# Turning the mixer's last token half by a transposing DMA instead of on TensorE

## The chip, the cores and the metric

The kernel runs on one core of one Trainium2 chip. The metric is the device time of one execution in microseconds; the median of three runs is taken. Engines are named as in the profile: PE is TensorE (matmuls; PEld its weight loads), DVE is VectorE, ACT is ScalarE, POOL is GpSimd, and SP is the engine whose queue issues most DMAs.

## The reference

The model is an encoder of two layers over 512 tokens of width 1024, in float32. Each layer is a half-step SwiGLU block, a mixer, and another half-step SwiGLU block; a final RMSNorm ends it. Only the mixer matters here:

```python
def mixer(h, w_in, gate_bias, rpb, w_na_out, w_f_out, w_o):
    z = h @ w_in
    ...
    y_na = neighbourhood_attention(q.reshape(shp), k.reshape(shp), v.reshape(shp), rpb) @ w_na_out
    y_f = fourier_mix(uf) @ w_f_out
    g_na = jax.nn.sigmoid(ga + gate_bias[0])
    g_f = jax.nn.sigmoid(gf + gate_bias[1])
    return (g_na * y_na + g_f * y_f) @ w_o
```

The change is about the last line: the gated sum, and its product with `w_o`.

## The kernel before

Every product is done in float32 by splitting each operand into a high and a low part and summing three matmuls (high by high, high by low, low by high). ACT copies the high part out (`whi` for weights, `m1h` and so on for activations), DVE subtracts to get the low part (`wlo`, `m1l`).

Large products are done by Strassen's scheme with seven half-size products, numbered 1 to 7. The gated sum is 512 tokens by 1024 features. It is cut into four quarters: features i = 0 or 1 (512 each) by tokens j = 0 or 1 (256 each). As the product with `w_o` needs the features on the partitions, each quarter is turned from tokens by features into features by tokens; the turned quarter is the tile `mq[i, j]`, in the code m00, m01, m10 and m11. The factors of the seven products are

- 1: m00; 5: m00 - m01; 2: m10; 6: that difference + m11; 7: m01 - m11; 3: m11; 4: m10 - (the factor of 6).

`combo` (L578) makes such a sum on DVE, and `parts` (L332, L333) splits it. `product` runs one of the seven over two weight granules of 12 matmuls each (L521, L522, L524); before a granule `ws.next` prepares weights up to two granules ahead: ACT writes `whi` (L199, or L194 where a sign is turned), DVE writes `wlo` (L202, L195), and some granules are first summed with another one on DVE (L172). `whi` and `wlo` have three buffers each, so a granule's copy waits until PE has done with the granule three before it. `put` (L1833) adds a finished bank of a product to the residual `x` on DVE, bank by bank. The products run in the order 1 (bank pair wA), 5 (wB), 2 (wC), 6 and 7 (both adding on into wA), 3 (into wB), 4 (into wA).

There are two ways to turn a quarter. Those of the first features, m00 and m01, go by DMA: `apart` separates the 16-bit words of the float32 values by two ACT copies (L357, tile `zs`) and issues a transposing DMA on the SP queue (L363, tile `zt`); `joined_words` puts the words together again by two ACT copies (L376). Those of the second features go by PE: `to_channels` runs eight transposes into PSUM (L1511) and two ACT evictions (L1512). The quarter (1, 1), the second features' second token half, is turned in a hook of the product wA, between its two granules; the quarter (1, 0) behind it. Ahead of this, `merge(1, ga1, w, j)` finishes a half: PE multiplies the attention rows with their output weights, DVE multiplies by the gate (L1499) and adds the Fourier part (L1500).

The order on each engine is made by a planner before the run. It lists the instructions in time by its own estimates, the earlier one in the program going first where two are ready. Where the code says `manual_schedule` for an engine, its order is that of the program: here PE and DVE from the product with the factor of 6 to that of 3, so on DVE the update of wC's first bank, the next weight part, the updates of wA's two banks, and so on. Each engine runs its list in order; an instruction that waits holds up those behind it. Weight loads go through the SP queue into nine raw buffers (L148); a load waits until its buffer is free. POOL issues DMAs that add one weight granule onto another (L158, L204).

Of the kernel before, what the change touches and what calls it, by code (L numbers as in the profile page):

```python
# [9 lines left out]
F32 = mybir.dt.float32  # L10
# [5 lines left out]
ALU = mybir.AluOpType  # L16
# [75 lines left out]
def encoder_kernel(  # L92
# [15 lines left out]
    def nm(s):  # L108
        uid[0] += 1
        return f"{s}_{uid[0]}"  # L110

    def slot(dt=F32, s="k", shape=(4, 256)):
        return kp.tile([P, *shape], dt, tag="k", name=nm(s), bufs=23)
# [5 lines left out]
    def bank(s="ps"):  # L119
        return pp.tile([P, T], F32, tag="ps", name=nm(s))  # L120

    def pair(s="ps"):
        return [bank(s), bank(s)]
# [228 lines left out]
    def words_apart(z):  # L352

        s = slot(U16, "zs", (2, 4, 2, P))
        words = z.bitcast(U16).rearrange("p b (q f h) -> p h q b f", q=4, h=2)
        for h in range(2):
            S.activation(s[:, h], words[:, h], AF.Copy)  # L357
        return s

    def turned_words(s):  # L360

        t = slot(U16, "zt", (2, 4, 256))
        nc.sync.dma_start_transpose(  # L363
            out=t.rearrange("p h q (b t) -> p (h q b) t", b=2), in_=s.rearrange("p h q b f -> p (h q b f)")
        )
        return t

    def apart(z):

        return turned_words(words_apart(z))  # L370

    def joined_words(to, t):

        to = to.bitcast(U16).rearrange("p i (t w) -> p w i t", w=2)
        for w in range(2):
            S.activation(to[:, w], t[:, w], AF.Copy)  # L376
# [140 lines left out]
    def late_low(parts, again=False):  # L517


        for ps, lh, ll, rh, _, start, _ in parts:  # L520
            PE.matmul(ps, lh, rh, start=start, stop=False, skip_group_check=again)  # L521
            PE.matmul(ps, ll, rh, start=False, stop=False, skip_group_check=again)  # L522
        for ps, lh, _, _, rl, _, stop in parts:
            PE.matmul(ps, lh, rl, start=False, stop=stop, skip_group_check=again)  # L524

    def product(ps, acts, kts, start, stop=True, again=False, hook=None, by_block=False, ahead=AHEAD):

        h, l, off = acts  # L530
        n = (len(kts) + 1) // 2

        def granule(i, w, b):
            res = []
            for k, kt in enumerate(kts[2 * i : 2 * i + 2]):
                c, z = slice(off + b * P, off + (b + 1) * P), slice(k * T, (k + 1) * T)
                res.append((
                    ps[b], h[:, kt, c], l[:, kt, c], w[0][:, z], w[1][:, z], start and i + k == 0,
                    stop and 2 * i + k == len(kts) - 1,
                ))  # L540
            return res

        if by_block:
            w = [ws.next() for _ in range(n)]
            for b in range(2):
                for i in range(n):
                    late_low(granule(i, w[i], b), again)
            return
        for i in range(n):
            w = ws.next(AHEAD if i < n - 1 and ahead else ahead)  # L550
            if i < n - 1:
                late_low(granule(i, w, 0) + granule(i, w, 1), again)
            else:
                late_low(granule(i, w, 0), again)
                late_low(granule(i, w, 1), again)
            if hook and i == 0:
                hook()
# [19 lines left out]
    def combo(dst, in0, in1, op, s):  # L577
        V.tensor_tensor(dst, in0, in1, op)  # L578
        return parts(dst, s)

    def parts(src, s):
        h, l = slot(F32R, s + "h"), slot(F32R, s + "l")
        split(h, l, src)
        return h, l, 0

    K4 = list(range(4))
# [499 lines left out]
    def stage_mixer(l, norm, nxt):  # L1086
# [310 lines left out]
        def rows_of(src, tb, w, kts=range(4), ps=None):  # L1397

            ps = bank() if ps is None else ps
            t = slice(tb * P, (tb + 1) * P)  # L1400
            for kt in kts:
                h_, l_ = src[kt]
                wh, wl = w[kt // 2]
                c = slice((kt % 2) * T, (kt % 2 + 1) * T)
                mm3(ps, h_[:, t], l_[:, t], wh[:, c], wl[:, c], kt == 0, kt == 3)
            return ps
# [87 lines left out]
        def merge(i, ga, w, j):  # L1494

            for b in range(2):
                ps = rows_of(o, 2 * j + b, w)
                g = ga[j][:, b, :]
                V.scalar_tensor_tensor(g, g, 1.0, ps, ALU.add, ALU.mult)  # L1499
            V.tensor_tensor(ga[j], ga[j], fs[i, j], ALU.add)  # L1500

        mq = {}

        def to_channels(i, ga, j):
            mq[i, j] = slot(F32, "mq")
            for q in range(2):
                tr = bank("tr").rearrange("p (a b) -> p a b", a=2)
                for k in range(2):
                    for b in range(2):
                        d = (2 * q + k) * P  # L1510
                        PE.transpose(tr[:, k, b * P : (b + 1) * P], ga[j][:, b, d : d + P], ident)  # L1511
                S.activation(mq[i, j][:, 2 * q : 2 * q + 2, :], tr, AF.Copy)  # L1512
# [26 lines left out]
        with tc.manual_schedule(engines={mybir.EngineType.DVE, mybir.EngineType.Activation}):  # L1539
            with tc.manual_schedule(engines={mybir.EngineType.PE}):  # L1540
                u, k1, pa, sb, acts4 = proj_UV()
# [235 lines left out]
        def taken(j):  # L1777
            turned[j] = apart(ga0[j])

        def channels(j):  # L1780
            mq[0, j] = slot(F32, "mq")
            joined_words(mq[0, j], turned[j])

        ga1 = gate_block(
            1, bias, acts, {1: lambda: taken(1), 5: lambda: taken(0), 2: lambda: channels(1), 7: lambda: channels(0)}
        )
        m00, m01 = mq[0, 0], mq[0, 1]
        a1 = parts(m00, "m1")
        a5 = combo(m00, m00, m01, ALU.subtract, "m5")
        w = [ws.next(), ws.next()]  # L1790
        merge(1, ga1, w, 1)
        merge(1, ga1, w, 0)
        pa = pair("wA")
        product(pa, a1, K4, True, hook=lambda: to_channels(1, ga1, 1))
        put(pa, 0, 0, -1)
        m11 = mq[1, 1]
        to_channels(1, ga1, 0)
        m10 = mq[1, 0]
        a6 = combo(m00, m00, m11, ALU.add, "m6")
        a2 = parts(m10, "m2")  # L1800
        pb = pair("wB")
        product(pb, a5, K4, True)
        put(pb, 1, 1, -1)
        V.tensor_tensor(m01, m01, m11, ALU.subtract)
        a7 = parts(m01, "m7")
        a3 = parts(m11, "m3")
# [22 lines left out]
    def put(ps, i, j, sign, bs=(0, 1)):  # L1829

        for b in bs:
            v = x[:, 2 * j + b, i * T : (i + 1) * T]
            V.scalar_tensor_tensor(v, ps[b], 0.5 * sign, v, ALU.mult, ALU.add)  # L1833
# [43 lines left out]
    for l in range(L):  # L1877
        nxt = Norm(3 * l + 1)
        stage_ffn(norm, nxt, False)
        norm, nxt = nxt, Norm(3 * l + 2)  # L1880
        stage_mixer(l, norm, nxt)
        norm, nxt = nxt, Norm(3 * l + 3)
        stage_ffn(norm, nxt, l == L - 1)
        norm = nxt
# [148 lines left out]
```

## Time and profile before

| | |
|---|---|
| runs | 1848.32, 1848.39, 1849.78 us |
| median | 1848.39 us |
| the profiled execution | 1848.74 us |
| its span in the profile | 1847.0 us |
| granted TensorE clock | 0.998 |
| PE busy | 1835.7 us |
| DVE busy | 1602.6 us |
| ACT busy | 1312.3 us |

The span runs from the first instruction of the program to the last, so 1.74 us of the profiled execution lie around it. The mixer's end stands twice in it, once per layer: from about 557 to 606 us and from about 1472 to 1522 us. In the timelines a row gives the start, the time, the engine, the line, the operation, the tile written and the tiles read, and how many instructions of the kind are merged; in square brackets the idle time before it and what ended it. On ACT and DVE one operation may start a little before the one ahead has ended, so the cost of one in a full stretch is the distance from start to start.

### The profile page before, as it was taken

Reading aid. Unit: us, or ns where it says so; the run is one execution under the profiler, and the core shown is the slowest. Engines: PE = TensorE matmul, PEld = TensorE weight load, DVE = VectorE, ACT = ScalarE, POOL = GpSimd, SP = SyncE. Lnnn points to the kernel's source line nnn. Section 1 sums busy time; section 2 is a strip of 40 time slices with the busy share of each in tenths; the row PEclk is TensorE's granted clock in tenths of the full one; section 3 lists DMA queues with packets and bytes.
Section 4 is the critical chain, followed back from the end, with each engine's and each line's share of the span. In section 5 each row is a group of like instructions: output and inputs, shape, how many; then the busy total and the mean of one; then the engine's idle time right before and its main releaser. Section 6 shows DMA issues by size and latency. Waiting matters only on the chain.

```text
span 1847.0 us, 24568 instructions
## 1 busy us (share of the span) xinstructions
PE 1835.7 (99%) x8850; PEld 1529.2 (83%) x8850; DVE 1602.6 (87%) x1942; ACT 1312.3 (71%) x1777; POOL 175.6 (10%) x215
## 2 busy tenths in 40 slices
PE   9999999999999999999999999999999999999998
PEld 7888888888888888888888888888888888888886
DVE  7878899786989987789998888997869899887898
ACT  6777875668676777787666778766776776777865
POOL 0001011100111010001010100101001101010010
PEclk9999999999999999999999999999999999999999
DMA  9898798933896789879888897989258966888695
GB/s 300 227 231 223 192 271 267 230 118 121 232 234 178 182 207 239 206 208 279 249 194 212 228 221 194 282 283 214 69 182 212 232 173 180 230 218 219 197 278 159
DMA packets 198378, 395.72 MB, mean 214 GB/s; under 512 B 103856, under 2 KB 103984, under 8 KB 198256
## 3 DMA queue, kind: packets, MB, share of 16 engines
q1 hardware_dynamic: 168912, 294.23, 49.9%
q0 software_dynamic: 28912, 99.38, 30.1%
q8 instruction: 69, 1.13, 0.2%
q10 hardware_dynamic: 432, 0.55, 0.1%
q14 instruction: 53, 0.43, 0.1%
HBM read 367.88 MB, written 2.11 MB: 200 GB/s over the span
## 4 chain that ended last, share of the span: by engine, by line
PE 94%; DVE 3%; issue 1%; DMA 1%; ACT 0%; POOL 0%; SPq 0%; DVEq 0%; ACTq 0%; POOLq 0%
PE A L521 10%; PE A L524 10%; PE A L522 10%; PE o L524 6%; PE o L521 6%; PE o L522 6%; PE B L521 5%; PE B L522 5%; PE B L524 5%; PE ps L326 4%; PE ps L327 3%; PE ps L328 3%; PE C L521 3%; PE C L522 3%; PE C L524 3%
## 5 line engine op out<-in xcount | busy, mean ns | idle before, releaser
L202 DVE TENSOR_TENSOR wlo<-raw,whi 128x1024 fp32r<-128x1024 f32 (+1 forms) x532 | 630.9, 1196 | 174.4 <-ACT whi L199 173.5
L199 ACT ACTIVATE whi<-raw 128x1024 fp32r<-128x1024 f32 (+1 forms) x532 | 544.0, 1033 | 263.4 <-PE A L522 53.6
L158 POOL DMA_DIRECT2D raw<-in_wst_dram x166 | 145.1, 898 | 1283.1 <-DMA raw<-in_wst_dram 530.5
L172 DVE TENSOR_TENSOR raw<-raw,raw 128x1024 f32<-128x1024 f32 (+1 forms) x148 | 177.0, 1196 | 2.0
L522 PE MATMUL A<-whi,xl 128*128 128x512 f32 x400 | 155.7, 389 | 0.0
L521 PE MATMUL A<-whi,xh 128*128 128x512 f32 x400 | 155.7, 389 | 0.0
L376 ACT ACTIVATE at<-zt 128x1024 uint16<-128x1024 uint16 (+2 forms) x96 | 110.3, 1166 | 15.1 <-DMA zt<-zs 15.0
L194 ACT ACTIVATE whi<-raw 128x1024 fp32r<-128x1024 f32 (+1 forms) x83 | 85.3, 1034 | 45.8 <-issue 12.5
L524 PE MATMUL A<-wlo,xh 128*128 128x512 f32 x400 | 115.0, 389 | 0.0
L195 DVE SCALAR_TENSOR_TENSOR wlo<-raw,whi 128x1024 fp32r<-128x1024 f32 (+1 forms) x83 | 98.6, 1198 | 13.1 <-ACT whi L194 13.1
L524 PEld LDWEIGHTS A<-wlo,xh 128*128 128x128 f32 x400 | 75.1, 188 | 15.5
L522 PEld LDWEIGHTS A<-whi,xl 128*128 128x128 f32 x400 | 75.1, 188 | 15.4
L521 PEld LDWEIGHTS A<-whi,xh 128*128 128x128 f32 x400 | 75.1, 188 | 15.4
L521 PE MATMUL C<-whi,xh 128*128 128x512 f32 x208 | 81.1, 390 | 0.2 <-ACT whi L199 0.2
L522 PE MATMUL C<-whi,xl 128*128 128x512 f32 x208 | 81.0, 389 | 0.0
L522 PE MATMUL B<-whi,xl 128*128 128x512 f32 x208 | 81.0, 389 | 0.0
L521 PE MATMUL B<-whi,xh 128*128 128x512 f32 x208 | 80.9, 389 | 0.0
L357 ACT ACTIVATE zs<-th 128x1024 uint16<-128x1024 uint16 x80 | 79.5, 1042 | 1.0 <-DVE th L766 0.9
L759 ACT ACTIVATE th<-sn,rh 128x512 f32<-128x512 f32 x80 | 55.1, 716 | 35.0 <-DVE sn L596 34.2
L591 ACT ACTIVATE sn<-A 128x512 f32<-128x512 f32 x104 | 59.2, 585 | 24.2 <-PE A L524 24.2
L524 PE MATMUL C<-wlo,xh 128*128 128x512 f32 x208 | 59.8, 389 | 0.0
L524 PE MATMUL B<-wlo,xh 128*128 128x512 f32 x208 | 59.8, 389 | 0.0
(429 smaller groups left out, 4686.6 us busy)
## 6 DMA issues: line engine op xcount, KB each, us to landing
raw<-in_wst_dram SPq DMA_DIRECT2D x468, 512.0 KB, 6.1
raw<-in_wst_dram POOLq DMA_DIRECT2D x176, 512.0 KB, 8.0
bm<-in_bias_dram SPq DMA_DIRECT2D x16, 512.0 KB, 4.1
raw<-in_wst_dram SPq DMA_DIRECT2D x30, 256.0 KB, 4.5
x<-in_xin_dram SPq DMA_DIRECT2D x4, 512.0 KB, 10.2
raw<-in_wst_dram POOLq DMA_DIRECT2D x8, 256.0 KB, 8.2
dft<-in_dft_dram POOLq DMA_DIRECT2D x8, 256.0 KB, 10.6
gb<-in_gbias_dram SPq DMA_DIRECT2D x4, 512.0 KB, 9.2
```

What stands on the lines that cost most here:

```text
L158: G.dma_start(out=self.t, in_=wst[GRAN_AT[self.plus]][:, 0 : self.n], accum_op=ALU.add)
L172: V.tensor_tensor(self.raw.t, self.raw.t, self.add.t, ALU.add)
L194: S.activation(hi, t, AF.Copy, scale=-1.0)
L195: self.last = V.scalar_tensor_tensor(lo, t, -1.0, hi.bitcast(F32), ALU.mult, ALU.subtract)
L199: S.activation(hi[:, cs], t[:, cs], AF.Copy)
L202: self.last = V.tensor_tensor(lo[:, cs], t[:, cs], hi[:, cs].bitcast(F32), ALU.subtract)
L326: PE.matmul(ps, lh, rh, start=start, stop=False, skip_group_check=again)
L357: S.activation(s[:, h], words[:, h], AF.Copy)
L376: S.activation(to[:, w], t[:, w], AF.Copy)
L521: PE.matmul(ps, lh, rh, start=start, stop=False, skip_group_check=again)
L522: PE.matmul(ps, ll, rh, start=False, stop=False, skip_group_check=again)
L524: PE.matmul(ps, lh, rl, start=False, stop=stop, skip_group_check=again)
```

## The change

The quarter (1, 1) is turned by the transposing DMA. Its words are taken apart right behind its `merge`, ahead of the other half's; the hook on the product wA goes. The words are joined behind the product wB and its update. The sum and the split for the factor of 6, which need m11, move there from their place ahead of the split of m10. This is done in both layers.

```diff
@@ -1789,18 +1789,20 @@
         a5 = combo(m00, m00, m01, ALU.subtract, "m5")
         w = [ws.next(), ws.next()]
         merge(1, ga1, w, 1)
+        t11 = apart(ga1[1])
         merge(1, ga1, w, 0)
         pa = pair("wA")
-        product(pa, a1, K4, True, hook=lambda: to_channels(1, ga1, 1))
+        product(pa, a1, K4, True)
         put(pa, 0, 0, -1)
-        m11 = mq[1, 1]
         to_channels(1, ga1, 0)
         m10 = mq[1, 0]
-        a6 = combo(m00, m00, m11, ALU.add, "m6")
         a2 = parts(m10, "m2")
         pb = pair("wB")
         product(pb, a5, K4, True)
         put(pb, 1, 1, -1)
+        m11 = slot(F32, "mq")
+        joined_words(m11, t11)
+        a6 = combo(m00, m00, m11, ALU.add, "m6")
         V.tensor_tensor(m01, m01, m11, ALU.subtract)
         a7 = parts(m01, "m7")
         a3 = parts(m11, "m3")
```

## The prediction

> **What bounds the kernel now.** I read the page first, then the timelines of PE, DVE and ACT around the mixer's end of the first layer, then the table by stretches for both layers, then the waits of the SP queue.
>
> ```profile
> PE 1835.7 (99%) x8850; PEld 1529.2 (83%) x8850; DVE 1602.6 (87%) x1942; ACT 1312.3 (71%) x1777; POOL 175.6 (10%) x215
> PE 94%; DVE 3%; issue 1%; DMA 1%; ACT 0%; POOL 0%; SPq 0%; DVEq 0%; ACTq 0%; POOLq 0%
> 557.00:585.70 28.70, 28.70 (x135) 23.58 (x134) 28.70 (x31) 17.20 (x20) 2.59 (x3) 1.00 0.55 129
> 1472.50:1501.20 28.70, 28.62 (x134) 23.47 (x134) 28.70 (x31) 17.20 (x20) 1.95 (x3) 1.00 0.53 128
> ```
>
> The first two rows (engines; the chain that ended last) say that PE bounds the kernel as a whole: busy 99%, 94% of the chain. So each microsecond of work taken off PE looks like a microsecond won. The last two (a stretch of the mixer's end in each layer; columns: stretch and its length, then busy time and count of PE, PEld, DVE, ACT, POOL) say something else about the place of the change. There DVE is busy 28.70 of 28.70 us, with 31 instructions and no gap, in both layers. PE and DVE are both full; ACT has 11.5 us free.
>
> PE's rows there, first of each group:
>
> ```profile
> 562.11 0.39 PE L521 MATMUL wA<-whi,m1h 128*128 128x512 f32 x1
> ...
> 564.83 1.04 PE L1511 MATMUL tr<-ident,sn 128*128 128x128 f32 x8
> 565.63 0.49 PE L521 MATMUL wA<-whi,m1h 128*128 128x512 f32 x1
> ...
> 568.50 1.04 PE L1511 MATMUL tr<-ident,sn 128*128 128x128 f32 x8
> ...
> 574.86 0.61 PE L521 MATMUL wC<-whi,m2h 128*128 128x512 f32 x2
> ...
> 580.57 0.39 PE L521 MATMUL wA<-whi,m6h 128*128 128x512 f32 x1
> ...
> 586.01 0.39 PE L521 MATMUL wA<-whi,m7h 128*128 128x512 f32 x1
> ```
>
> And DVE's, from the sum of the second token half (L1500) on:
>
> ```profile
> 560.43 1.22 DVE L1500 TENSOR_TENSOR sn<-sn,fs 128x1024 f32<-128x1024 f32 x1
> ...
> 567.30 1.22 DVE L578 TENSOR_TENSOR mq<-mq,mq 128x1024 f32<-128x1024 f32 x1
> 568.43 1.28 DVE L1833 SCALAR_TENSOR_TENSOR x<-wA,x 128x512 f32<-128x512 f32 x2
> 569.63 1.22 DVE L202 TENSOR_TENSOR wlo<-raw,whi 128x1024 fp32r<-128x1024 f32 x1
> 570.76 1.22 DVE L172 TENSOR_TENSOR raw<-raw,raw 128x1024 f32<-128x1024 f32 x1
> 571.90 1.22 DVE L333 TENSOR_TENSOR m6l<-mq,m6h 128x1024 fp32r<-128x1024 f32 x1
> 573.03 1.22 DVE L202 TENSOR_TENSOR wlo<-raw,whi 128x1024 fp32r<-128x1024 f32 x1
> 574.17 1.22 DVE L333 TENSOR_TENSOR m2l<-mq,m2h 128x1024 fp32r<-128x1024 f32 x1
> 575.30 1.28 DVE L1833 SCALAR_TENSOR_TENSOR x<-wB,x 128x512 f32<-128x512 f32 x2
> 576.50 1.22 DVE L1804 TENSOR_TENSOR mq<-mq,mq 128x1024 f32<-128x1024 f32 x1
> 577.63 1.22 DVE L172 TENSOR_TENSOR raw<-raw,raw 128x1024 f32<-128x1024 f32 x1
> 578.77 1.22 DVE L202 TENSOR_TENSOR wlo<-raw,whi 128x1024 fp32r<-128x1024 f32 x1
> 579.90 1.23 DVE L333 TENSOR_TENSOR m7l<-mq,m7h 128x1024 fp32r<-128x1024 f32 x1
> 581.04 1.23 DVE L333 TENSOR_TENSOR m3l<-mq,m3h 128x1024 fp32r<-128x1024 f32 x1
> 582.17 1.23 DVE L202 TENSOR_TENSOR wlo<-raw,whi 128x1024 fp32r<-128x1024 f32 x1
> 583.31 0.69 DVE L1833 SCALAR_TENSOR_TENSOR x<-wC,x 128x512 f32<-128x512 f32 x1
> 583.91 1.22 DVE L202 TENSOR_TENSOR wlo<-raw,whi 128x1024 fp32r<-128x1024 f32 x1
> 585.04 0.69 DVE L1833 SCALAR_TENSOR_TENSOR x<-wA,x 128x512 f32<-128x512 f32 x1
> 586.21 0.69 DVE L1833 SCALAR_TENSOR_TENSOR x<-wA,x 128x512 f32<-128x512 f32 x1 [0.47 <-PE wA L524]
> ```
>
> The reader is to see three things. A full DVE operation costs 1.13 to 1.14 us from start to start. The update from wC's first bank runs at 583.31, though wC was over at 580.57: DVE is about 3 us behind PE. And it catches up only at 586.21, with its first gap (0.47 us). The seventh product (m7) adds into the banks of wA, so it cannot begin before the update of wA's first bank at 585.04 has ended at 585.73; it began at 586.01. DVE is late by almost as much as PE is.
>
> **Part 1: PE loses eight transposes per layer.** The group at 564.83 lasts 0.80 us to the next row. The granule behind it lasts 2.87 us (565.63 to 568.50) where the one ahead took 2.72 (562.11 to 564.83), so the switch costs 0.15 more: 0.95 us. wC takes 5.71 us (574.86 to 580.57) instead of twice 2.72; the 0.27 us is the wait for m2l, which ends at 574.17 + 1.22 = 575.39. With m6 moved behind it, m2l no longer queues behind m6l and this wait goes. On PE's own account: 1.22 us per layer. The new times: wA ends at 567.55, the transposes that remain run to 568.34, wB ends at 573.9, wC at 579.35, m6 at 584.8.
>
> **Part 2: what ACT and the DMA queue get.** The nearest rows are those of the first features' halves, which already go this way, some 40 us earlier in this layer, and ACT's own around the change:
>
> ```profile
> L357 ACT ACTIVATE zs<-fs x4: 1049/1050/1057, 517.8 to 524.3; 128x1024 uint16<-128x1024 uint16 x4
> DMA to landing us min/median/max: 4.4/4.6/4.7
> L376 ACT ACTIVATE mq<-zt x8: 1348/1359/1367, 527.2 to 1455.8; 128x1024 uint16<-128x1024 uint16 x8
> 560.99 1.06 ACT L194 ACTIVATE whi<-raw 128x1024 fp32r<-128x1024 f32 x1 [1.74 <-PE ps L328]
> ...
> 565.47 1.09 ACT L1512 ACTIVATE mq<-tr 128x512 f32<-128x512 f32 x2 [0.24 <-PE tr L1511]
> ...
> 568.24 1.06 ACT L199 ACTIVATE whi<-raw 128x1024 fp32r<-128x1024 f32 x1 [1.68 <-PE wA L522]
> ...
> 571.48 1.06 ACT L199 ACTIVATE whi<-raw 128x1024 fp32r<-128x1024 f32 x1 [0.26 <-ACT m6h L332]
> ```
>
> ACT loses the two evictions (1.09 us) and gains two copies apart (2 x 1.05) and two joins (2 x 1.36): 3.7 us more, into the 11.5 us that it has free. The sum of L1500 is there at 561.65; ACT is free at 562.05; the copies end at about 564.0. The weight copies due in these two microseconds move back by as much; their granules belong to wB, which starts at 568.3, so that is hidden. The transposing DMA lands 4.4 to 4.7 us after its issue: 568.4 to 568.7. I take 568.6. Then ACT has, in program order, the weight copy freed by wA (568.24 less 0.95 = 567.3), two evictions to 569.3, m2h to 570.2, the first join to 571.5, the weight copy freed by wB (571.48 less 0.95, ready at 570.5) to 572.5, the second join to about 573.8. So m11 is ready at 573.8, not at 566.6.
>
> The Trainium skill, VectorE: DVE Perf Modes, "The three transpose paths", has a rule against the change: a 128x128 two-byte transpose is 390 ns on TensorE and 1309 ns by the DMA crossbar. Taken block after block, my estimate by that page is 16 x 1.309 = 20.9 us, a landing at 585 and some 12 us lost per layer. The landing row above, for a tile of the same shape, gives 4.4 to 4.7 us for all sixteen, so the trace speaks against it and the sum goes by the row.
>
> **Part 3: DVE loses nothing.** No DVE operation is added or removed. Five depend on m11 and move behind 573.8: m6's sum (567.30), m6l (571.90), the difference (576.50), m7l (579.90) and m3l (581.04). What can fill the place from 567.30 on: both updates of wA (1.2), the weight parts of 569.63 and 573.03, the raw sums of 570.76 and 577.63, m2l, and the updates of wB (1.2), together 2 x 1.2 + 5 x 1.14 = 8.1 us, up to 575.4. m11 is there 1.6 us earlier, so DVE need not stand idle. It then does m6's sum, the difference, m6l (done at about 578.8, before wC's end at 579.35), m7l, m3l and the two weight parts of 578.77 and 582.17; the first of these may come about 1 us late for m6's products. The sum of the work ahead of wA's update is the same, so that update again starts at 585.04 and ends at 585.73. m7's product starts at about 585.8 instead of 586.01. Gain: 0.2 us per layer, 0.4 in both; the other 1.0 us per layer becomes PE waiting for DVE. Behind this point PE has no wait in these rows that could give more back; m3's weights, which wait for a POOL accumulation started by a weight part that now comes some 2 us later, still have the length of m7's product (5.4 us) as cover.
>
> The unknown cost is how long DVE stands still for m11. Below: if m3l falls behind wA's update, DVE gives back 1.1 us and PE keeps its 1.22 us per layer. Above: the transposing DMA is queued on SP in the planner's order, and a load there waits long:
>
> ```profile
> SPq L148 <- DVE wlo L202: 38.2, 9, 18.1
> ```
>
> That 18.1 us wait ends with the weight part of 569.63, which in the new order is done at about 569.7. A transposition behind that load is issued at about 570.0, lands at 574.7 and is joined at 577.3; behind the next one, whose place the raw sum of 570.76 frees, it is joined some 1.2 us later, at 578.5. DVE, in order, then idles 1.9 to 3.1 us from 575.4. I take the near end, m11 at 573.8, since the transposition is ready at 564.0, more than 5 us before that load may go.
>
> The sum is against the profiled execution: 1848.74 us (span 1847.0 and 1.74 around it), less 0.4 is 1848.3. The median of the runs shown is 0.35 lower, so the forecast is 1848.39 - 0.4 = 1848.0 us.
>
> **The rivals.**
> - PE's gain is kept. For it: PE is 94% of the chain. Against: DVE's 28.70 of 28.70. It needs m3l or another full operation to slip behind 585.04. 2 x 1.22 = 2.4 us: 1846.0.
> - m11 somewhat late: ACT waits in order for the landing, or the planner puts the joins behind more weight copies. Every microsecond by which the second join ends after 575.4 is one of DVE idle. With 1 to 1.9 us per layer, less the 0.2: +1.6 to +3.4 us, 1850.0 to 1851.8.
> - Slower: the transposition behind the waiting load on SP, as worked out. Price 1.9 to 3.1 us per layer less 0.2, so +3.4 to +5.8: 1851.8 to 1854.2. It decides from a join that ends after 577.3. The 18.1 us wait speaks for it; that the load's place comes free more than 5 us after the copies apart, against it.
> - The planner orders much else anew, either way by over 4 us: nothing in these rows asks for it.
>
> **How the numbers follow.** Forecast (within about 1 us of 1848.0) 0.45; PE's gain kept 0.12; m11 somewhat late 0.16; behind the load 0.19; all anew 0.08, two thirds of it slower. About 0.2% (3.7 us) is what a measurement of this kernel can tell from no change. Faster by more: 0.03. Slower by more: 0.05 and seven eighths of 0.19, 0.22. Within: 0.75. The range goes from 1845.8, just under the second case, to 1853.0, the middle of the fourth: it leaves out half of that and the last case, 0.18 in all.
>
> **What would show it.** Right: eight rows L1511 per layer fewer, a landing near 568.6, the second join's end before 575.4, DVE still full to wA's first update, PE with about 1 us of waiting for weight parts or updates in m6 and m7, m7's product about 0.2 us earlier. Wrong: DVE gaps before m6's sum (m11 late), an SP wait ahead of the transposition, or m7's product earlier by 1 us with m3l behind wA's update.

## The result, and the profile after

| | before | after |
|---|---|---|
| median, us | 1848.37 (6 runs, 1847.75 to 1849.78) | 1858.22 (6 runs, 1854.55 to 1862.12) |
| the profiled execution, us | 1848.74 | 1857.54 |
| its span, us | 1847.0 | 1855.8 |
| granted TensorE clock | 0.998 | 0.999 |

The change makes the kernel slower: ratio 1.0051, 95% interval 1.0040 to 1.0062, 9.85 us by the medians. The prediction said 1848.0 us, with 1853.0 as its upper end. Three far slower runs (2030.7 and 3098.7 us, one each in experiments 2 and 4, and 10627.66 us, one of the kernel before) are left out of all times below.

The page after, first the engines, then the chain that ended last:

```profile
PE 1835.3 (99%) x8834; PEld 1527.2 (82%) x8834; DVE 1602.5 (86%) x1942; ACT 1317.7 (71%) x1781; POOL 176.0 (9%) x215
PE 91%; DVE 4%; DMA 3%; ACT 1%; issue 1%; POOL 0%; SPq 0%; ACTq 0%; DVEq 0%; POOLq 0%
```

The sixteen transposes are gone (8850 instructions to 8834), DVE has the 1942 it had, ACT four more. PE's share of the chain fell from 94% to 91%; DVE and DMA have one and two points more of it. No engine has more work that could explain 9 us. So the loss is waiting, and the table of waits says for what. PE's waits at the mixer's end of the first layer (550 to 612 us), before and then after; columns: who waits, at which product, for whom; total, number and longest in us:

```profile
PEld wC L522 <- DVE m2l L333: 0.4, 1, 0.4
PEld wA L521 <- DVE x L1833: 0.3, 1, 0.3
```

```profile
PEld tr L433 <- DVE x L1835: 2.8, 1, 2.8
PEld wA L524 <- DVE wlo L202: 2.4, 1, 2.4
PEld wA L522 <- DVE m4l L333: 1.0, 1, 1.0
PEld wA L521 <- DVE x L1835: 0.3, 1, 0.3
```

Three waits are new: for a weight part in product 6 (L524, 2.4 us on the load side), for the low part m4l in product 4, and, behind that, for an update of `x` at the transposes for the next block (tr, L433). The second layer has the first and the last of these again at 2.3 and 2.8. PE's timeline after, at the same places, shows what PE itself lost:

```profile
578.56 0.39 PE L521 MATMUL wA<-whi,m6h 128*128 128x512 f32 x1
...
582.53 1.20 PE L524 MATMUL wA<-wlo,m6h 128*128 128x512 f32 x4 [1.99 <-DVE wlo L202]
...
599.23 0.50 PE L522 MATMUL wA<-whi,m4l 128*128 128x512 f32 x1 [0.55 <-DVE m4l L333]
...
604.59 0.98 PE L433 MATMUL tr<-ident,x 128*128 128x128 f32 x7 [2.44 <-DVE x L1835]
```

**Wait 1, in product 6.** DVE after, from its gap on:

```profile
562.96 1.23 DVE L195 SCALAR_TENSOR_TENSOR wlo<-raw,whi 128x1024 fp32r<-128x1024 f32 x1 [0.78 <-ACT whi L194]
...
573.85 1.21 DVE L578 TENSOR_TENSOR mq<-mq,mq 128x1024 f32<-128x1024 f32 x1
...
575.58 1.21 DVE L1806 TENSOR_TENSOR mq<-mq,mq 128x1024 f32<-128x1024 f32 x1
576.72 1.22 DVE L333 TENSOR_TENSOR m6l<-mq,m6h 128x1024 fp32r<-128x1024 f32 x1
577.85 1.22 DVE L172 TENSOR_TENSOR raw<-raw,raw 128x1024 f32<-128x1024 f32 x1
578.99 1.22 DVE L333 TENSOR_TENSOR m7l<-mq,m7h 128x1024 fp32r<-128x1024 f32 x1
580.12 1.22 DVE L333 TENSOR_TENSOR m3l<-mq,m3h 128x1024 fp32r<-128x1024 f32 x1
581.26 2.35 DVE L202 TENSOR_TENSOR wlo<-raw,whi 128x1024 fp32r<-128x1024 f32 x2
...
585.26 0.68 DVE L1835 SCALAR_TENSOR_TENSOR x<-wA,x 128x512 f32<-128x512 f32 x1
```

Both weight parts of product 6 now stand behind m7l and m3l. Before, their order was part, m7l, m3l, part (578.77, 579.90, 581.04, 582.17). So it is the first part that has moved, behind two splits. Before, m7's high part was done at 578.81, just after the first weight part had begun, which fits that part going ahead. After, m7h and m3h are ready earlier than the weights are (ACT's rows below), and being earlier in the program they go first. That is a reading by the measured times: the planner goes by its own estimates, and those are not on record. PE got to L524 of product 6 at 580.54 (582.53 less 1.99); the part it needed ended at 581.26 + 1.22 = 582.48.

**Waits 2 and 3, behind product 3's weights.** The weight part of each granule of product 6 releases a DMA on POOL (L204), which adds another granule onto the raw buffer for product 3. That line's answer for the first layer's end, before and after: start of the first and the last, then the time from issue to landing:

```profile
L204 POOL DMA_DIRECT2D raw<-in_wst_dram x2: 860/864/869, 581.0 to 583.9; - x2
DMA to landing us min/median/max: 5.3/5.3/5.3
```

```profile
L204 POOL DMA_DIRECT2D raw<-in_wst_dram x2: 869/1044/1220, 583.7 to 584.2; - x2
DMA to landing us min/median/max: 5.4/7.2/9.0
```

Before, the two were issued 2.9 us apart and each landed 5.3 us later. After, the two parts run one right behind the other, the two DMAs are issued 0.5 us apart, and the second lands 9.0 us after its issue. ACT's weight copies (L199) show it, before and after:

```profile
586.41 1.06 ACT L199 ACTIVATE whi<-raw 128x1024 fp32r<-128x1024 f32 x1 [1.65 <-DMA raw<-in_wst_dram]
...
589.38 1.06 ACT L199 ACTIVATE whi<-raw 128x1024 fp32r<-128x1024 f32 x1 [1.13 <-DMA raw<-in_wst_dram]
```

```profile
570.64 2.58 ACT L376 ACTIVATE mq<-zt 128x1024 uint16<-128x1024 uint16 x2
...
576.83 1.06 ACT L332 ACTIVATE m7h<-mq 128x1024 fp32r<-128x1024 f32 x1 [0.67 <-DVE mq L1806]
577.80 1.04 ACT L332 ACTIVATE m3h<-mq 128x1024 fp32r<-128x1024 f32 x1
...
589.21 1.06 ACT L199 ACTIVATE whi<-raw 128x1024 fp32r<-128x1024 f32 x1 [4.24 <-DMA raw<-in_wst_dram]
...
593.37 1.06 ACT L199 ACTIVATE whi<-raw 128x1024 fp32r<-128x1024 f32 x1 [2.49 <-DMA raw<-in_wst_dram]
```

The first row of the second fence is the pair of joins, of which more below. The copies for product 3 moved from 586.41 and 589.38 to 589.21 and 593.37. On DVE the second weight part stands ahead of m4's sum and m4l in the order written by hand, and the planner has put wA's updates between those two and wB's last update behind them. DVE before, then after:

```profile
590.48 1.23 DVE L202 TENSOR_TENSOR wlo<-raw,whi 128x1024 fp32r<-128x1024 f32 x1 [0.71 <-ACT whi L199]
...
599.87 0.68 DVE L1833 SCALAR_TENSOR_TENSOR x<-wB,x 128x512 f32<-128x512 f32 x1
```

```profile
594.46 1.23 DVE L202 TENSOR_TENSOR wlo<-raw,whi 128x1024 fp32r<-128x1024 f32 x1 [2.94 <-ACT whi L199]
...
597.95 1.23 DVE L333 TENSOR_TENSOR m4l<-mq,m4h 128x1024 fp32r<-128x1024 f32 x1
...
603.85 0.68 DVE L1835 SCALAR_TENSOR_TENSOR x<-wB,x 128x512 f32<-128x512 f32 x1
```

DVE idles 2.94 us for the late weights with other work behind it, and PE then waits for m4l and for that last update (604.59 against 603.85 + 0.68 = 604.53).

### The profile page after: what moved, and what is told of

It is laid out like the page before. It is cut to its first block, busy times and chain, and to the rows that moved or that the text cites. A ratio compares the mean times of both kernels' runs of the same rounds, so it can differ in the third digit from the quotient of the medians.

```text
span 1855.8 us, 24542 instructions
## 1 busy us (share of the span) xinstructions
PE 1835.3 (99%) x8834; PEld 1527.2 (82%) x8834; DVE 1602.5 (86%) x1942; ACT 1317.7 (71%) x1781; POOL 176.0 (9%) x215
## 4 chain that ended last, share of the span: by engine, by line
PE 91%; DVE 4%; DMA 3%; ACT 1%; issue 1%; POOL 0%; SPq 0%; ACTq 0%; DVEq 0%; POOLq 0%
PE A L521 10%; PE A L524 10%; PE A L522 10%; PE o L524 7%; PE o L521 7%; PE o L522 7%; PE B L521 5%; PE B L522 5%; PE B L524 5%; PE ps L326 4%; PE ps L327 3%; PE ps L328 3%; PE C L521 3%; PE C L522 3%; PE C L524 3%; DMA zt<-zs 1%
## 5 line engine op out<-in xcount | busy, mean ns | idle before, releaser
L199 ACT ACTIVATE whi<-raw 128x1024 fp32r<-128x1024 f32 (+1 forms) x532 | 543.3, 1033 | 260.9 <-PE A L522 52.2
L522 PE MATMUL A<-whi,xl 128*128 128x512 f32 x400 | 155.7, 389 | 0.0
L524 PE MATMUL A<-wlo,xh 128*128 128x512 f32 x400 | 115.0, 389 | 0.0
L524 PEld LDWEIGHTS A<-wlo,xh 128*128 128x128 f32 x400 | 75.1, 188 | 15.6
L522 PEld LDWEIGHTS A<-whi,xl 128*128 128x128 f32 x400 | 75.1, 188 | 15.4
L522 PE MATMUL C<-whi,xl 128*128 128x512 f32 x208 | 81.0, 389 | 0.0
L522 PE MATMUL B<-whi,xl 128*128 128x512 f32 x208 | 81.0, 389 | 0.0
L524 PE MATMUL C<-wlo,xh 128*128 128x512 f32 x208 | 59.8, 389 | 0.0
L524 PE MATMUL B<-wlo,xh 128*128 128x512 f32 x208 | 59.8, 389 | 0.0
```

The source lines that it names most:

```text
L199: S.activation(hi[:, cs], t[:, cs], AF.Copy)
```

## The experiments

All times are medians of several runs. The kernel before ran beside all of them: 1848.31 us in the 25 runs beside experiments 1 to 4, 1847.97 us in the 32 beside experiments 5 to 8. The ratios are those on record and can differ a little from the quotient of the medians.

**1. The kernel before, with only the weight parts put back.** PE still does all transposes; only DVE's order is made that of the kernel after.

```diff
+    low_gate = [None]
...
-                    self.last = V.tensor_tensor(lo[:, cs], ..., ALU.subtract)
+                    with tc.issue_after(low_gate[0]) if low_gate[0] else nullcontext():
+                        self.last = V.tensor_tensor(lo[:, cs], ..., ALU.subtract)
...
+        m3_low = V.tensor_tensor(l3, m11, h3.bitcast(F32), ALU.subtract)
...
+        low_gate[0] = m3_low.ins
         product(pc, a2, K4, True)
+        low_gate[0] = None
```

> The kernel before, with one thing changed: on DVE the two weight parts for product 6 stand behind m7l and m3l, as they do in the changed kernel; m11 is still turned by PE. Theory (order on DVE): those two weight parts start the two POOL accumulations that make product 3's weights, so these land some 4 us later, DVE waits for them in order, and m4l and the updates of wB come late: PE loses about 3.3 us per layer at product 4 and at the transposes of x behind it; product 6 itself starts late enough here to lose under 0.5 us. 1848.4 + 2 x 3.3 = 1855, range 1852 to 1858. Rival (the transposing DMA, its copies on ACT and its traffic cost the time): nothing of it is here, so 1848 to 1849.

Measured: 1855.88 us, ratio 1.0047 (1.0030 to 1.0063). Its DVE timeline, PE's waits in the first layer and the line of the accumulation (the edit moves the line numbers: L524 here is L522 above, L526 is L524, L435 is L433):

```profile
579.32 1.22 DVE L1810 TENSOR_TENSOR m3l<-mq,m3h 128x1024 fp32r<-128x1024 f32 x1
580.45 2.35 DVE L203 TENSOR_TENSOR wlo<-raw,whi 128x1024 fp32r<-128x1024 f32 x2
```

```profile
PEld tr L435 <- DVE x L1840: 2.8, 1, 2.8
PEld wA L524 <- DVE m4l L335: 1.0, 1, 1.0
...
PEld wA L526 <- DVE wlo L203: 0.3, 1, 0.3
```

```profile
DMA to landing us min/median/max: 5.4/7.2/9.1
```

With no transposing DMA for this quarter and no move of m11, the two late waits are there at the sizes of the kernel after, and so is most of its loss. Only the wait in product 6 is small, since PE with its transposes comes later. So one weight part moved behind two splits on DVE is alone enough for about 7.6 us.

**2. The kernel after, with the difference and both splits moved behind wC's product.**

```diff
-        V.tensor_tensor(m01, m01, m11, ALU.subtract)
-        a7 = parts(m01, "m7")
-        a3 = parts(m11, "m3")
         pc = pair("wC")
         product(pc, a2, K4, True)
+        V.tensor_tensor(m01, m01, m11, ALU.subtract)
+        a7 = parts(m01, "m7")
+        a3 = parts(m11, "m3")
```

> The changed kernel, with the difference for product 7 and the splits for 7 and 3 moved behind product 2 in the program, so that the weight parts for product 6 stand ahead of them on DVE; m11 still goes by the transposing DMA. Theory (order on DVE): the 2.1 us of product 6, the 0.3 to 0.9 us of m4l and the 2.7 us at the transposes of x are gone in both layers and PE keeps its 1.2 us per layer: 1846 to 1848.5. Rival (the transposing DMA and its traffic): it is all still here, so 1856 to 1859.

Measured: 1849.78 us, ratio 1.0005 (0.9995 to 1.0014). Of the 9.85 us lost 8.4 are won back, but not PE's gain; the expected time was lower. DVE's timeline says why:

```profile
583.28 1.23 DVE L333 TENSOR_TENSOR m7l<-mq,m7h 128x1024 fp32r<-128x1024 f32 x1
584.42 0.69 DVE L1835 SCALAR_TENSOR_TENSOR x<-wA,x 128x512 f32<-128x512 f32 x1
585.02 1.23 DVE L333 TENSOR_TENSOR m3l<-mq,m3h 128x1024 fp32r<-128x1024 f32 x1
586.15 0.69 DVE L1835 SCALAR_TENSOR_TENSOR x<-wA,x 128x512 f32<-128x512 f32 x1
```

m3l now stands between wA's two updates, and product 7 waits for each of them: PE's rows have 0.88 and 0.49 us, on the load side the table of waits has 1.3 and 0.9 (the first put down to ACT's m3h). m3l is not needed until product 3. The accumulations are as close here as in the kernel after (0.5 us apart, the second landing 9.1 us after its issue), but 3.1 us earlier, at 580.6 and 581.1, and PE's wait at the transposes is 0.9 us on the load side in the first layer and none in the second. So closeness alone costs little. This led to experiment 6.

**3. The kernel after, without the accumulations.**

```diff
-                    add(d, a, then=b.key if dma else None)
+                    add(d, a, then=b.key if dma and name("a") != "wa" else None)
```

> The changed kernel without the POOL accumulations behind the weight parts for product 6 in the output product: product 3 then runs with a weight granule that lacks one summand. Theory: the wait of product 6 for its weight part stays (2.1 us per layer), the waits at m4l and at the transposes of x go: 1848.4 + 2 x (2.1 - 1.2) = 1850.2, range 1848.5 to 1852, and the spread of the runs shrinks from 7.6 us to about 2. Rival (the transposing DMA itself): as the changed kernel, 1855 to 1859.

Measured: 1851.9 us, ratio 1.0020 (1.0010 to 1.0029), just inside the expected range and 1.7 us over its middle. PE's waits in the first layer:

```profile
PEld wA L524 <- DVE wlo L202: 2.4, 1, 2.4
PEld wA L521 <- DVE x L1835: 0.3, 1, 0.3
```

Waits 2 and 3 are gone with the accumulations, and 6.3 us with them; wait 1 stays whole. What missed: the runs were also expected to lie closer together, and still spread over 5.4 us.

The profiled execution has something that bears on both misses. PE stood 1.94 us for the weight part in the first layer, went on at 583.49, and from 585 to 588 us its granted clock was 0.50 to 0.52. From the end of the wait to product 7 took 5.38 us; in the kernel after, at full clock, it took 3.75. Less these 1.6 us the execution of 1851.7 would stand at 1850.1, an estimate, where 1850.2 was expected.

**4. The kernel before, with the sum for the factor of 6 moved, nothing else.**

```diff
-        a6 = combo(m00, m00, m11, ALU.add, "m6")
         a2 = parts(m10, "m2")
         ...
         put(pb, 1, 1, -1)
+        a6 = combo(m00, m00, m11, ALU.add, "m6")
```

> The kernel before with the factor of product 6 moved behind product 5 in the program as in the changed kernel, m11 still turned by PE. On DVE the first weight part for product 6 keeps its place ahead of m7l and m3l. Theory: as the kernel before, 1847.5 to 1849. Rival (moving the factor of 6 behind product 5 is what costs): 1854 to 1859.

Measured: 1848.62 us, ratio 1.0002 (0.9992 to 1.0011). The first weight part, at 578.39, kept its place ahead of m7l, at 579.52. The move by itself costs nothing that shows.

**5. The kernel after, without the first of the two accumulations.** If the second is slow because it queues behind the first, it must be faster alone.

```diff
-                    add(d, a, then=b.key if dma else None)
+                    add(d, a, then=b.key if dma and not (name("a") == "wa" and g == 0) else None)
```

> The changed kernel without the first of the two POOL accumulations of the output product; the second is kept. One of product 3's two weight granules then lacks a summand. Theory (the second accumulation is late because it queues behind the first, which the late weight part has pushed to within 0.5 us of it): alone it lands about 5.4 us after its issue instead of 9.0, so product 3's second weight part comes some 3.6 us earlier, and the waits at m4l and at the transposes of x shrink to under 0.5 us: as without both accumulations, 1850 to 1852.5. Rival (the second one is late by itself, its own weight part being late): 1854.5 to 1858.

Measured: 1851.84 us, ratio 1.0019 (1.0010 to 1.0028). The line of the accumulation, first layer:

```profile
DMA to landing us min/median/max: 6.3/6.3/6.3
```

The second alone landed after 6.3 us where with the first ahead of it it took 9.0 (5.4 against 8.6 in the second layer): 2.7 and 3.2 us of the delay go with the first. In the first layer it was still 1.0 us over the 5.3 of the kernel before, and PE's wait at the transposes was 1.3 us there, where under 0.5 was expected; in the second layer it was gone. So lateness alone costs little too: most of the loss in the kernel after takes a pair that is both late and close.

**6. The kernel after, with product 6's weights prepared first and m3 split late.**

```diff
+        ws.prep(ws.pos + 3)
         V.tensor_tensor(m01, m01, m11, ALU.subtract)
         a7 = parts(m01, "m7")
-        a3 = parts(m11, "m3")
...
                 put(pc, 0, 0, 1, (1,))
+                a3 = parts(m11, "m3")
```

> The changed kernel with product 6's first weight part prepared ahead of the factors of 7 and 3, and the split of m11 for product 3 moved behind the updates of wA. Theory (DVE is full, and the transposition's copies add an idle stretch of 0.8 us to it): one operation less stands between wA's two updates than in the reordered kernel, so PE gets back 0.7 us per layer of its 1.7 at product 7; the 1.0 us at the first update stays: 1848.0, range 1847.0 to 1849.0. Rival (PE's saving arrives whole once product 3's weights are in time): 1846.

Measured: 1847.24 us, ratio 0.9996 (0.9987 to 1.0005): in the expected range, and not to be told from the kernel before. All three new waits are gone. One wait on DVE is left between 557 and 585.7 us:

```profile
DVE wlo L195 <- ACT whi L194: 0.8, 1, 0.8
```

It is the gap at 562.96 in the kernel after: the first copy apart goes ahead of a weight copy on ACT, and DVE's next operation is that weight's low part. PE's timeline still has about 1 us of waiting at product 7 in each layer.

**7. The same, with the copies apart held behind the last weight copy.**

```diff
-                S.activation(hi, t, AF.Copy, scale=-1.0)
+                self.high = S.activation(hi, t, AF.Copy, scale=-1.0)
...
-        t11 = apart(ga1[1])
+        with tc.issue_after(ws.items[ws.prepped - 1].high.ins):
+            t11 = apart(ga1[1])
```

> As the kernel with the split for product 3 moved behind the updates of wA, and ACT's copies apart put behind the weight copy of the product wA's second granule, so that DVE does not wait 0.8 us for that. Theory (DVE sets the time here): both updates of wA come 0.8 us earlier, PE keeps about 1.0 of its 1.2 us per layer: 1846.4, range 1845.5 to 1847.5. Rival (DVE's idle stretch is covered elsewhere): no difference to the kernel without this, 1848.

Measured: 1846.15 us, ratio 0.9986 (0.9977 to 0.9995), faster than both kernels, if only by 0.10% against the kernel before when the medians are compared. The same stretch of the first layer in this kernel's table by stretches (PE, PEld, DVE, ACT, POOL: busy time and count), beside that of the kernel after:

```profile
557.00:585.70 28.70, 28.49 (x131) 23.32 (x130) 28.54 (x31) 20.43 (x23) 2.27 (x3) 1.00 0.68 153
```

```profile
557.00:585.70 28.70, 26.71 (x122) 21.86 (x121) 27.91 (x30) 20.32 (x22) 2.62 (x3) 1.00 0.56 131
```

DVE is busy 28.54 instead of 27.91 us, PE 28.49 instead of 26.71. In the timeline PE waits 0.37 us per layer at product 7 where it waited about 1.0 in experiment 6: closing DVE's gap of 0.8 us brought 0.6 us per layer. The medians lie 1.1 us apart, which is what two layers would give, but the runs of the two kernels overlap (1845.66 to 1850.23 and 1843.94 to 1848.43), so the times alone do not show it.

**8. The kernel before, with m3 split late.** Is it the late split alone that helps?

```diff
-        a3 = parts(m11, "m3")
...
+                a3 = parts(m11, "m3")
```

> The kernel before with only the split of m11 for product 3 moved behind the updates of wA; all transposes stay on PE. Theory (PE and DVE are level here): freeing DVE by one operation without taking work from PE wins at most the waits for wA's updates, 0.2 to 0.3 us per layer: 1848.0, range 1847.3 to 1848.6. Rival (DVE alone bounds the stretch): 1.1 us per layer, 1846.2.

Measured: 1849.7 us, ratio 1.0007 (0.9999 to 1.0016). No gain, against what was expected. The operation taken off DVE ahead of product 7 wins nothing while PE still has its transposes; in the first layer the profile has 0.8 us of waiting for `x` at the transposes instead. The median is 1.7 us over the kernel before, of which the table below places about half; the interval holds no change. So the rival of that experiment, that DVE alone bounds this stage, is out as well. DVE's relief alone (8) wins nothing, PE's relief with only the weight parts put first (2) wins nothing, both together (7) do.

**All runs by stage.** PE's time from product 1 (wA) to the first product behind the mixer, taken from the start of each product in the profiled executions: difference to the kernel before, sum of both layers, in us. Product 4 includes the transposes of `x` between its granules. The last column is the difference of the medians.

| | 1, 5 and 2 | 6 | 7 and 3 | 4 | sum | medians |
|---|---|---|---|---|---|---|
| after | -2.5 | 4.5 | 0.1 | 6.2 | 8.3 | 9.9 |
| 1 | 0.1 | 0.4 | 0.0 | 6.3 | 6.8 | 7.6 |
| 2 | -2.5 | 2.0 | 1.4 | 0.8 | 1.7 | 1.5 |
| 3 | -2.5 | 6.1 | 0.1 | 0.0 | 3.7 | 3.6 |
| 4 | -0.6 | 0.4 | -0.1 | 0.3 | -0.1 | 0.3 |
| 5 | -2.5 | 4.7 | 0.1 | 1.2 | 3.5 | 3.9 |
| 6 | -2.5 | 1.9 | -0.1 | 0.0 | -0.7 | -0.7 |
| 7 | -2.5 | 0.7 | -0.1 | 0.3 | -1.6 | -1.8 |
| 8 | 0.0 | 0.0 | 0.3 | 0.7 | 0.9 | 1.7 |

In every kernel with the transposing DMA PE is 2.5 us ahead at product 6; what becomes of it is settled behind that point. The 6.1 us of experiment 3 hold the 1.6 us at the low clock.

## Why the prediction was wrong

**Part 1 held.** In these two profiles PE was 0.82 us earlier than before at wA's start and 2.01 earlier at 578.56, the start of product 6 (580.57 before). So 1.19 us were won by then, as worked out, and 1.30 in the second layer.

**Part 2 held for the DMA.** These are the rows of the transposition in the first layer's end:

```profile
L363 SPq DMA_TRANSPOSE zt<-zs x1: 1338/1338/1338, 563.9 to 563.9; - x1
...
DMA to landing us min/median/max: 4.3/4.3/4.3
```

It was issued at 563.9 and landed at 568.2; the joins ended at 570.64 + 2.58 = 573.2, where the prediction had 573.8. Nothing on SP stood ahead of it, and DVE did not idle for m11. Both rivals about a late m11 are out, the slow one at 0.19 among them; what came is nearest to the last rival (much else ordered anew, 0.08), which had been dismissed for want of a row that asked for it. By the Trainium skill, VectorE: DVE Perf Modes, "The three transpose paths", sixteen blocks at its 1309 ns would, by estimate, land 20.9 us after the issue; the 4.3 us here speak against taking its figure block by block.

**Three steps failed, the last by most.**

1. *"The weight copies due in these two microseconds move back by as much; their granules belong to wB, … so that is hidden."* This named the use on PE as cover and forgot DVE's order. The prediction also had both copies apart behind the weight copy of 560.99; the first went ahead of it, at 560.92, and put it off to 561.88. Its low part is DVE's next operation, so DVE stood still 0.78 us (0.63 in the second layer) in a stretch where the prediction itself had shown it without a gap. "DVE loses nothing" fell here. Experiment 7 takes the gap away.
2. *"The first of these may come about 1 us late for m6's products."* The order was foreseen: m6l, m7l, m3l, then the two weight parts. The size was not: PE stood 1.99 us (1.84 in the second layer). By the prediction's own numbers the first part ends at 578.8 + 3 x 1.14 = 582.2; it ended at 582.48. But PE and DVE were both some 0.8 us earlier in this profile, and DVE gave that back in the gap of step 1. Counted from wA's start, product 7 began 1.09 us later than before (0.88 in the second layer), instead of 0.2 earlier.
3. *"m3's weights, which wait for a POOL accumulation …, still have the length of m7's product (5.4 us) as cover."* The delay of the issue was foreseen (2 us; 2.7 for the first). Two things were not: that bringing both weight parts together issues both accumulations together, so that the second lands after 9.0 instead of 5.3 us; and that DVE has m4's sum, wA's updates, m4l and wB's update queued behind the part that waits. The cover was computed for product 3 on PE alone, and there it held: product 3 did not wait. PE lost 0.87 us in the granule that needs m4l and 2.66 at the transposes of `x` in the first layer, 0.04 and 2.66 in the second: 6.2 us.

Together 1.09 + 0.88 + 6.2 = 8.2 us, of the 9.85 of the medians and 8.8 of the profiled executions. By the table, the prediction's sum allowed 2.0 us of waiting at product 6 (1.0 per layer), where 4.5 came, and nothing at product 4 and its transposes, where 6.2 came. From outside, experiment 3 takes 6.3 us away with the accumulations, and experiment 1 brings 7.6 us with the order alone.

**Open.** PE also lost 1.7 us between the two mixers' ends and was 0.8 us early ahead of the first; experiments 1 and 3 lose nothing there, and whether this belongs to the change was not shown. Why the runs of the kernel after spread over 7.6 us and those before over 2.0 is not settled; leaving out the accumulations did not end it. The granted clock bears on it. Only the kernels in which PE stands still for 1.8 us or more at a time in the mixer's end (after, 1, 3 and 5) have runs with a mean granted clock of 0.997, 9 of 30, and the slowest run of each is one of them; experiment 3 shows one such loss at half clock. That the waits cause it was not shown: the four such waits in the profile of the kernel after (1.84 to 2.44 us) were followed by no lower clock. A kernel in which the second accumulation goes by another queue was not tried.

## What to carry to other kernels

When an operation moves, an order planned by readiness changes for the others: list what each displaced operation releases, DMAs above all, and follow that to its last user on every engine, not only on the engine that sets the time. A cover has to be checked on each in-order engine that the waiting instruction stands in: here PE had 5.4 us to spare, and DVE had none. Where two engines are level, as here, relieving one won nothing until the other was relieved too: the transposing DMA cost 0.51% as made, and with DVE's order mended it brought 0.14% (0.05 to 0.23).

## What was unexpected of the hardware

Two accumulating DMAs of 512 KB from POOL took 5.3 us each when issued 2.9 us apart, and 5.4 and 9.0 us when issued 0.5 us apart. Over all profiles the first of a pair took 5.3 to 5.5 us, and the second the longer the closer it followed: 9.0 to 9.1 us at 0.5 us apart (after, experiments 1 and 2), 7.5 to 8.7 at 0.9 (their second layers), 6.6 to 7.9 at 1.4 or 1.5 (6, 7 and 8), 5.9 to 6.0 at 2.0 to 2.3 (their second layers), 5.3 to 5.5 at 2.9 to 3.7 (before and 4). The later one without the first took 6.3 and 5.4 (5). So a close pair behaves nearly as if one went after the other. Other transfers ran at the same time, and their part in it was not separated.

The granted clock fell to 0.50 for some 3 us in the middle of a kernel, once in the ten profiles (experiment 3), 1.5 us after PE had gone on from a wait of 1.94 us.
